# A branch for overflow blocks moved ahead of the last regular block, with its loads on GpSimd's queue, and norm rows spread by products

## The chip, the cores and the metric

The kernel runs on one core of one Trainium2 chip. Its time is the device time of one execution in microseconds (us). The core has five instruction streams: TensorE (PE, whose weight loads have their own row PEld), VectorE (DVE), ScalarE (ACT), GpSimd (POOL) and SyncE (SP). Here SP computes nothing; it issues nearly all transfers from HBM.

## The reference

Two decoder layers on 256 tokens of width 1024, in float32. Layer 0 mixes tokens by block attention, layer 1 by a gated MLP (gMLP); each layer then has a mixture of experts. After each part x is normalised with a row `g` and a row `b`.

```python
def grouped_expert_ffn(xf, expert_id, gates, w1, w3, w2):
    # assignments sorted by expert; each block of rows run by its own expert
    def run_block(args):
        rows, e = args
        h = jax.nn.silu(rows @ w1[e]) * (rows @ w3[e])
        return h @ w2[e]
    ...
def reference(x, ...):
    for i in range(DEPTH):                      # 2 layers
        h = moba_attention(...) if i % 2 == 0 else chunked_gmlp(...)
        x = layer_norm(DEEPNORM_ALPHA * x + h, ln1_g[i], ln1_b[i])
        h = hier_moe(...)                       # 64 experts, 2 per token
        x = layer_norm(DEEPNORM_ALPHA * x + h, ln2_g[i], ln2_b[i])
    return x
```

Each expert has three matrices of 1 MB (w1 and w3, packed as two pieces `w13`, and `w2`). All 64 experts of a layer are read, 201 MB a layer.

## The kernel before

**Slots.** Weights and large activations live in a ring of 24 slots of 8 KB a partition (1 MB each). `slot()` takes the slot that was given up first, `slot(True)` the one given up last. A load into a slot waits until whatever used the slot is done.

**Blocks.** In `moe` expert 0 runs on all tokens; the other 63 are taken four at a time, each on up to 32 gathered rows. That makes NB = 16 regular blocks, numbered 0 to 15, the last one with three experts. A block gathers its rows by one-hot products (`gather`, L625), works out gates (`scatter`, L635), does the up products (`up`, L666), silu and product (`mid`, L674 and L675), a transpose (L756), the down products (L762), copies them out of PSUM (`copy`, L104 on DVE, L106 on ACT in turn), and adds the result to four PSUM banks `acc` by products (`back`, L774). Block b+1 is gathered ahead of block b's down products.

**Overflow.** An expert with more than 32 rows needs more blocks. How many there are is known only at run time, in the last element of the integer tile `li`. Up to four further blocks are written as nested `tc.If` bodies (`tail`, L825), each of them on all engines. With these inputs no such block runs: every engine jumps over the four bodies. The branch stands behind the last regular block (L823 reads the count, L828 branches). Its body holds the loads of the extra experts, so SP branches too. On the path that is not taken each engine waits for its own semaphores (SP for those of its transfers) and advances them as the body would have.

**Order.** A scheduler sets the order within each engine; what is inside a `tc.If` does not mix with what is outside. Instructions of an engine run in that order. `keep_warm(2)` issues two 128x512 products that nobody reads (L115): once in the last block, and in layer 0 once more behind the branch. Then comes the norm: statistics (L192), aggregates (L201), a reciprocal root by POOL (L187), and two passes on DVE (L206 subtracts and multiplies by the g row, L207 multiplies and adds the b row). In layer 0 the result is transposed on PE (L231) and the gMLP's first products (L378) follow. The rows come through `load_ln` (L179, L180): two transfers of 512 KB, each a row of 4 KB repeated to 128 partitions, queued on SP behind the last block's weights.

The helpers `copy`, `bank` and `keep_warm`, and the constants `ones` and `ident`, are defined above these functions; pool psB ("B") has two PSUM banks, psA ("A") two, psY ("Y") four.

Of the kernel before, what the change touches and what calls it, by code (L numbers as in the profile page):

```python
# [16 lines left out]
PSUM = bass.MemoryType.PSUM  # L17
SP = mybir.EngineType.SP

P = 128  # L20
D = 1024
# [8 lines left out]
NE = 64  # L30
# [4 lines left out]
NB = -(-NMAIN // 4)  # L35
NTAIL = 4
NBT = NB + NTAIL
STAT = 8
# [12 lines left out]
def trunk(ctx: ExitStack, tc: tile.TileContext, t, out):  # L51
    nc = tc.nc
# [9 lines left out]

    # Everything of 8 KB a partition lives in these slots, weight pieces and activations alike. A piece takes
    # the slot that was given up first, so that it is loaded as far ahead as the slots reach; what is written
    # shortly after it takes its slot may have the one given up last.
    idle = deque(range(RING))
# [43 lines left out]

    # TensorE's clock falls back when it waits; products that nobody reads keep it up until there is work
    def keep_warm(n):
# [3 lines left out]

# [1 line left out]
    xT_slot = slot()  # L118
# [7 lines left out]

# [1 line left out]
    ident = const.tile([P, P], F32, name="ident")  # L128
# [21 lines left out]
    iota_t = ramp([P, T], [[1, T]], 0, 0, "iota_t")  # L150
    # places of the static blocks' rows, by expert; further down, what keeps them out of the others
    iota_s = ramp([P, CAP * STAT], [[1, CAP * STAT]], FAR, 0, "iota_s")
# [13 lines left out]
    iota80 = ramp([NE, 4 * NBT], [[1, 4 * NBT]], 0, 0, "iota80")  # L166
    # dense: experts run on all tokens; stat: experts whose first block has a place known beforehand
    dense = const.tile([NE, 1], F32, name="dense")
# [8 lines left out]
    def load_ln(g, b, l):  # L177
# [3 lines left out]
        return gb  # L181

    def rsqrt(var):
        ve = small.tile([P, 1], F32, tag="ve", name="ve")
        nc.vector.tensor_scalar(ve, var, EPS, None, op0=OP.add)  # L185
        r = small.tile([P, 1], F32, tag="rs", name="rs")
        nc.gpsimd.tensor_tensor(r, ve, mhalf, op=OP.pow)  # L187
        return r
# [4 lines left out]

    # x <- LN(s) for one tile of tokens, s in two halves; each half goes on to `then` as it is ready
    def after(i):
# [15 lines left out]

    # x <- LN(ALPHA * x + acc)
    def close(x, a, acc, gb, then):
# [21 lines left out]

# [1 line left out]
    def attention(xT_slot, x):  # L237
        xT = by_k(xT_slot)
        with tc.tile_pool(name="att", bufs=1) as att, tc.tile_pool(name="att2", bufs=2) as att2:
# [10 lines left out]
            def qkv(g, w):  # L250
                y = ys[g % 2]
                qT = y[:, 0:1024].rearrange("p (c j t) -> p c j t", c=2, j=2)
                kT = y[:, 1024:1536].rearrange("p (c t) -> p c t", c=2)
                v = y[:, 1536:2048].rearrange("p (a f) -> p a f", a=NT)
                # two heads share the partitions: each has its own copy of q, with zeros for the other's
                nc.gpsimd.memset(qT[64:, :, 0, :], 0.0)
                nc.gpsimd.memset(qT[:64, :, 1, :], 0.0)
                for i in range(2):
                    wt = by_k(w[i])
                    for c in range(2):  # L260
                        ps = bank(psA, "A")
                        for kc in range(KC):
                            nc.tensor.matmul(ps[:, :T], wt[:, kc, c * P:(c + 1) * P], xT[:, kc, :],  # L263
                                             start=(kc == 0), stop=(kc == KC - 1))
                        if i == 0:
                            nc.scalar.mul(qT[:64, c, 0, :], ps[:64, :T], SCALE)
                            nc.scalar.mul(qT[64:, c, 1, :], ps[64:, :T], SCALE)
                        else:
                            nc.vector.tensor_copy(kT[:, c, :], ps[:, :T])
                    drop(w[i])  # L270
                wt = by_k(w[2])
                for a in range(NT):
                    ps = bank(psA, "A")
                    for kc in range(KC):
                        nc.tensor.matmul(ps[:, :256], xT[:, kc, a * P:(a + 1) * P], wt[:, kc, :],
                                         start=(kc == 0), stop=(kc == KC - 1))
                    nc.scalar.copy(v[:, a, :], ps[:, :256])
                drop(w[2])
                return qT, kT, v
# [72 lines left out]

# [1 line left out]
    def gmlp(xT_slot, x):  # L354
        xT = by_k(xT_slot)
        with tc.tile_pool(name="gm", bufs=1) as gm, tc.tile_pool(name="gm2", bufs=2) as gm2:
# [35 lines left out]

            # the first tile of tokens goes ahead while the second is still being closed
            ld = [v_load(cb) for cb in range(2)]
# [89 lines left out]

# [1 line left out]
    def moe(l, xT_slot, x, then):  # L486
        xT = by_k(xT_slot)
        with tc.tile_pool(name="mr", bufs=1) as mr:
# [22 lines left out]

            # the dense experts' first products run while the routing is worked out
            def dense_up(e):
# [63 lines left out]

            # a token's rank among its expert's, and its place if that is in a static block
            ab = new(NE, "ab", BF16)
# [34 lines left out]

            # a block's slot: one-hots (later h and its transpose), gates, gathered rows (later the output)
            def gather(b, m=None):
# [12 lines left out]

            # where a block's rows go back to, and how much they weigh there  # L630
            def scatter(m, oh, xg):
# [10 lines left out]

            def load(src, regs, into=None, parts=1):
                ws = [slot() for _ in regs] if into is None else into
                n = 2048 // parts
                for i in range(parts):
                    for w, e in zip(ws, regs):
                        nc.sync.dma_start(w[:, i * n:(i + 1) * n], src[bass.ds(e, 1), :, i * n:(i + 1) * n])
                return ws

            def block_regs(b):
                n = NMAIN - STARTS[b] if b == NB - 1 else 4
                s0 = STARTS[b]
                if s0 + n <= STAT:
                    return [ND + s0 + j for j in range(n)]
                return [nc.values_load(li[0:1, s0 + j:s0 + j + 1], engines=(SP,), min_val=0, max_val=NE - 1)
                        for j in range(n)]
# [21 lines left out]
            first = gather(0, m0)  # L679
            # each expert's first block after the static ones, and the places there  # L680
            rank, sd = sl, em
# [15 lines left out]
            nc.vector.tensor_add(end, base, ex)  # L697
            # which expert each block is of
            mb = mr.tile([NE, 4 * NBT], F32, name="mb")
# [29 lines left out]
            pa = up(first[2], first_half)  # L729
            # gates  # L730
            dg = new(EG, "dg")
# [19 lines left out]

            # one half of a block's output, and its way back to the tokens
            def down(h, hT, ye, w, gT, first=False, last=False, extra=False):
# [24 lines left out]
            for b in range(NB - 1):  # L778
# [6 lines left out]
                if b == 0:  # L785
                    dw2 = piece(t["w2"][l, 0])
                if b == NB // 2:
                    for a in range(NT):
                        for n in range(2):
                            nc.tensor.matmul(acc[a][n], alpha, x[:, a, n * 512:(n + 1) * 512], start=False, stop=False)  # L790
# [9 lines left out]
                drop(*w2, mine)  # L800

            mine, xg, gT, h, hT, ye = nxt
            regs = block_regs(NB - 1)
# [4 lines left out]
            for n in range(2):  # L808
                for w, e in zip(w2, regs):
                    nc.sync.dma_start(by_c(w)[:, :, n * 512:(n + 1) * 512],  # L810
                                      t["w2"][l, bass.ds(e, 1)].rearrange("e p (c n) -> (e p) c n", c=2)
                                      [:, :, n * 512:(n + 1) * 512])
            gb = load_ln("ln2_g", "ln2_b", l)
            down(h, hT, ye, w2, gT, last=True)
# [5 lines left out]

            # blocks beyond the regular ones
            own = [slot() for _ in range(5)]
            more = nc.values_load(li[0:1, 4 * NBT:4 * NBT + 1], min_val=0, max_val=4 * NBT)  # L823

            def tail(b):  # L825
                if b == NBT:
                    return
                with tc.If(more > STARTS[b] - STAT):  # L828
                    _, xg, gT, h, hT, ye = scatter(*gather(b, own[0]))
                    regs = block_regs(b)  # L830
                    mid(up(xg, lambda half: load(t["w13"][l, half], regs, own[1:]), False), h)
                    down(h, hT, ye, load(t["w2"][l], regs, own[1:]), gT, extra=True)
                    tail(b + 1)
                    if b == NB:
                        for a in early:
                            stats(acc[a], st[a])

            tail(NB)
            if l < DEPTH - 1:
                keep_warm(2)  # L840
            drop(*own)
            last = None
# [70 lines left out]
```

## Time and profile before

| what | us |
|---|---|
| median of 3 runs (lowest, highest) | 1359.46 (1357.36, 1360.37) |
| span of the profiled execution, first to last instruction | 1356.7 |
| PE busy in it | 1248.2 (92%) |
| DVE, ACT, POOL busy | 273.3, 118.8, 16.0 |
| SP's transfers, share of the 16 DMA engines' span | 84.1% |

The profiled execution has no other time of its own than its span, so differences are worked out in the span and laid on the median of the runs; 2.8 us lie between the two. The page's 40 slices show DMA at 420 GB/s through most of both mixtures of experts, and at 127 to 188 GB/s in the gMLP, where PE is busy throughout. In the rows, "x62" counts records; a float32 product leaves two records on PE and two on PEld. An entry such as [2.59 <-PEq L828] is idle time of the engine before the row and what ended it; a q behind an engine's name is its instruction sequencer.

### The profile page before, as it was taken

How to read it: one execution, taken by the hardware profiler on the slowest of the kernel's cores; microseconds unless marked ns; L12 is line 12 of the kernel's file. 1: busy time of each engine (PE TensorE's matmuls, PEld its weight loads, DVE VectorE, ACT ScalarE, POOL GpSimd, SP SyncE). 2: the span in 40 equal slices, each digit the busy share in tenths (PEclk: the TensorE clock that was granted, in tenths of full speed). 3: DMA queues.
4: the chain of work that ended last, by engine and by line, in shares of the span. 5: the costliest groups of instructions: out<-in, count | busy, mean ns of one | idle time of the engine just before them, and what ended most of it. 6: DMA issues, size and time to landing. Idle time of an engine off the chain costs nothing. (4 is left out here: it accounts for less than half of the span.)

```text
span 1356.7 us, 16421 instructions
## 1 busy us (share of the span) xinstructions
PE 1248.2 (92%) x6442; PEld 614.5 (45%) x6442; DVE 273.3 (20%) x721; ACT 118.8 (9%) x273; POOL 16.0 (1%) x45
## 2 busy tenths in 40 slices
PE   8999999988898888889999999999998889888885
PEld 7776554433333333324456666655433324333331
DVE  1322531111111111003231111352111111111102
ACT  1321100000000000001010000020000000000000
POOL 2000000000000000000000000000000000000000
PEclk9999999999999999999999999999999999999998
DMA  9936389999999999998943444449999999999995
GB/s 361 420 148 227 126 336 421 421 421 420 421 422 420 421 422 420 421 388 356 419 175 127 184 152 158 188 157 422 420 421 421 421 421 421 422 421 420 421 420 225
DMA packets 71014, 469.02 MB, mean 346 GB/s; under 512 B 8080, under 2 KB 8080, under 8 KB 16784
## 3 DMA queue, kind: packets, MB, share of 16 engines
q1 hardware_dynamic: 69056, 464.55, 84.1%
q10 hardware_dynamic: 1872, 3.32, 0.7%
q8 instruction: 54, 0.88, 0.3%
q14 instruction: 32, 0.26, 0.1%
HBM read 466.79 MB, written 1.05 MB: 345 GB/s over the span
## 5 line engine op out<-in xcount | busy, mean ns | idle before, releaser
L666 PE MATMUL A<-s,s 128*32 128x512 f32 x2048 | 307.5, 602 | 29.0 <-DMA s<-in_w 29.0
L762 PE MATMUL B<-s,s 128*32 128x512 f32 x1024 | 190.6, 598 | 30.7 <-DMA s<-in_w 15.3
L666 PEld LDWEIGHTS A<-s,s 128*32 128x32 f32 x2048 | 70.9, 110 | 215.2 <-issue 150.1
L625 PEld LDWEIGHTS B<-s,s 128*128 128x128 f32 x1024 | 118.9, 192 | 43.8 <-issue 22.0
L625 PE MATMUL B<-s,s 128*128 128x128 f32 x1024 | 128.7, 280 | 0.0
L774 PE MATMUL Y<-s 128*128 128x512 f32 x256 | 118.9, 606 | 1.9 <-ACT s L106 1.5
L104 DVE COPY s<-B 128x512 f32<-128x512 f32 x64 | 44.2, 691 | 365.5 <-PE B L625 196.8
L762 PEld LDWEIGHTS B<-s,s 128*32 128x32 f32 x1024 | 45.6, 109 | 155.9 <-issue 81.5
L438 PE MATMUL A<-s,s 128*128 128x256 f32 x384 | 90.1, 379 | 0.0
L426 PE MATMUL Y<-s,scr 128*128 128x512 f32 x192 | 87.7, 601 | 0.2 <-DVE scr L460 0.2
L106 ACT COPY s<-B 128x512 f32<-128x512 f32 x64 | 37.5, 586 | 519.7 <-PE B L762 271.4
L774 PEld LDWEIGHTS Y<-s 128*128 128x128 f32 x256 | 45.8, 189 | 75.6 <-issue 63.4
L438 PEld LDWEIGHTS A<-s,s 128*128 128x128 f32 x384 | 71.1, 190 | 17.2 <-issue 9.3
L263 PE MATMUL A<-s,s 128*128 128x256 f32 x256 | 64.0, 396 | 5.4 <-DMA s<-in_wqkv 5.4
L263 PEld LDWEIGHTS A<-s,s 128*128 128x128 f32 x256 | 48.9, 199 | 14.9 <-issue 8.7
L426 PEld LDWEIGHTS Y<-s,scr 128*128 128x128 f32 x192 | 34.7, 190 | 40.0 <-issue 35.2
L675 DVE TENSOR_TENSOR s<-s,A 128x256 f32<-128x256 f32 x32 | 13.4, 420 | 160.8 <-ACT s L674 160.8
L378 PE MATMUL A<-s,s 128*128 128x512 f32 x96 | 43.1, 593 | 0.0
L378 PE MATMUL B<-s,s 128*128 128x512 f32 x96 | 42.8, 592 | 0.0
L611 DVE TENSOR_TENSOR s<-iota_t,sm 128x256 f32<-128x256 f32 (+1 forms) x56 | 21.1, 413 | 102.0 <-PE A L666 102.0
L674 ACT ACTIVATE s<-A 128x256 f32<-128x256 f32 x32 | 12.3, 384 | 307.3 <-PE A L666 291.7
L756 PE MATMUL A<-ident,s 128*128 128x128 f32 x64 | 13.8, 297 | 24.3 <-DVE s L675 24.3
(190 smaller groups left out, 703.8 us busy)
## 6 DMA issues: line engine op xcount, KB each, us to landing
s<-in_w SPq DMA_DIRECT2D x372, 1024.0 KB, 19.8
s<-in_w SPq DMA_DIRECT2D x24, 512.0 KB, 11.3
s<-in_wv SPq DMA_DIRECT2D x12, 1024.0 KB, 11.1
s<-in_wu SPq DMA_DIRECT2D x12, 1024.0 KB, 8.8
s<-in_wout SPq DMA_DIRECT2D x12, 1024.0 KB, 9.1
s<-in_wqkv SPq DMA_DIRECT2D x11, 1024.0 KB, 18.1
s<-in_wo SPq DMA_DIRECT2D x4, 1024.0 KB, 19.9
s<-in_ln_g SPq DMA_DIRECT2D x4, 512.0 KB, 10.8
```

What stands on the lines that cost most here:

```text
L104: nc.vector.tensor_copy(o, i)
L106: nc.scalar.copy(o, i)
L263: nc.tensor.matmul(ps[:, :T], wt[:, kc, c * P:(c + 1) * P], xT[:, kc, :], start=(kc == 0), stop=(kc == KC - 1))
L378: nc.tensor.matmul(ps, xT[:, kc, a * P:(a + 1) * P], by_k4(w[kc // 4])[:, kc % 4, :], start=(kc == 0), stop=(kc == KC - 1))
L426: nc.tensor.matmul(acc[a][h], mx[:, a, :], by_c(wo)[:, i % 2, h * 512:(h + 1) * 512], start=(i == 0), stop=(i == NCH - 1))
L438: nc.tensor.matmul(pu[:, :T], by_k(w)[:, kc, j * P:(j + 1) * P], xT[:, kc, :], start=(kc == 0), stop=(kc == KC - 1))
L611: nc.vector.tensor_tensor(oh[i][:, :, :n], over(at, n), s.to_broadcast([P, NT, n]), op=OP.is_equal)
L625: nc.tensor.matmul(ps[:, k * P:(k + 1) * P], x[:, a, kc * P:(kc + 1) * P], oh[2][:, a, :], start=(a == 0), stop=(a == NT - 1))
L666: nc.tensor.matmul(pa[32 * j:32 * j + 32, :], xg[:, kc, 32 * j:32 * j + 32], by_k4(w[min(j, len(w) - 1)])[:, k, :], start=(kc == 0), stop= ...
L756: nc.tensor.transpose(pt[:, c * P:(c + 1) * P], h[:, c * P:(c + 1) * P], ident)
L762: nc.tensor.matmul(py[32 * j:32 * j + 32, :], hT[:, c, 32 * j:32 * j + 32], by_c(w[min(j, len(w) - 1)])[:, c, n * 512:(n + 1) * 512], star ...
L774: nc.tensor.matmul(acc[a][n], gT[:, a * P:(a + 1) * P], ye[:, n * 512:(n + 1) * 512], start=first, stop=last, skip_group_check=extra)
```

## The change

1. `tail(NB)` and the reservation of its five slots move ahead of block 15's up products. The slots are now the five given up last. The recomputation of statistics inside the body goes, since the statistics now always come after it.
2. The body's transfers and its register loads are issued by GpSimd (POOL) instead of SP.
3. `load_ln` for this norm is replaced by `row_ln` in block 12 (two transfers of 4 KB to one partition) and `spread` in block 13: four products of a column of ones with 512 elements of the row, each copied from PSUM over the 128 partitions of the slot. The register with the count is read in block 12 too.

```diff
+    def row_ln(g, b, l):
+        gb = slot()
+        nc.sync.dma_start(gb[0:1, :D], t[g][l:l + 1, :])
+        nc.sync.dma_start(gb[0:1, D:], t[b][l:l + 1, :])
+        return gb
+
+    def spread(gb):
+        for i in range(4):
+            sl = slice(i * 512, (i + 1) * 512)
+            ps = bank(psB, "B")
+            nc.tensor.matmul(ps, ones[0:1, :], gb[0:1, sl], start=True, stop=True)
+            copy(gb[:, sl], ps)
...
+                if b == NB - 4:
+                    gb = row_ln("ln2_g", "ln2_b", l)
+                    more = nc.values_load(li[0:1, 4 * NBT:4 * NBT + 1], min_val=0, max_val=4 * NBT)
+                if b == NB - 3:
+                    spread(gb)
...
+            own = [slot(True) for _ in range(5)]
+
+            def tail(b):
+                if b == NBT:
+                    return
+                with tc.If(more > STARTS[b] - STAT):
+                    _, xg, gT, h, hT, ye = scatter(*gather(b, own[0]))
+                    regs = block_regs(b, POOL)
+                    mid(up(xg, lambda half: load(t["w13"][l, half], regs, own[1:], dma=nc.gpsimd), False), h)
+                    down(h, hT, ye, load(t["w2"][l], regs, own[1:], dma=nc.gpsimd), gT, extra=True)
+                    tail(b + 1)
+
+            tail(NB)
+            drop(*own)
+
             mine, xg, gT, h, hT, ye = nxt
             regs = block_regs(NB - 1)
             pa = up(xg, lambda half: load(t["w13"][l, half], regs, parts=1 + half))
...
-            gb = load_ln("ln2_g", "ln2_b", l)
             down(h, hT, ye, w2, gT, last=True)
...
-            # blocks beyond the regular ones
-            own = [slot() for _ in range(5)]
-            more = nc.values_load(li[0:1, 4 * NBT:4 * NBT + 1], min_val=0, max_val=4 * NBT)
...
-            tail(NB)
             if l < DEPTH - 1:
                 keep_warm(2)
-            drop(*own)
```

The line numbers after the change are 15 or 16 higher: L666 is L681, L774 is L789, L762 is L777, L115 is L116, L206 is L221.

PE between block 14 and block 15 of layer 0, before (block 14's last products L774, block 15's first, the two unread ones):

```order
L774 MATMUL Y<-s_3195 128x512 x4
L666 MATMUL A<-s_3447,s_3354 32x512
L115 MATMUL A<-ones 128x512 x2
L666 MATMUL A<-s_3448,s_3354 32x512
L666 MATMUL A<-s_3449,s_3354 32x512 x2
```

The same place on PE now; the rows left out are the four bodies, over which PE jumps:

```order
L789 MATMUL Y<-s_3224 128x512 x4
L804 TENSOR_LOAD li
L828 COMPARE_AND_BRANCH
...
L828 UNCONDITIONAL_BRANCH x5
L681 MATMUL A<-s_4069,s_3383 32x512
L116 MATMUL A<-ones 128x512 x2
L681 MATMUL A<-s_4070,s_3383 32x512
L681 MATMUL A<-s_4071,s_3383 32x512 x2
```

The read of the count and the branch now stand between block 14's last product and block 15's first.

PE at the end of layer 0's mixture of experts, before, from block 15's transposes to the gMLP's first products:

```order
L756 MATMUL A<-ident,s_3354 128x128 x2
L762 MATMUL B<-s_3499,s_3354 32x512
L762 MATMUL B<-s_3500,s_3354 32x512
L762 MATMUL B<-s_3501,s_3354 32x512 x2
...
L774 MATMUL Y<-s_3354 128x512 x2
L823 TENSOR_LOAD li
L828 COMPARE_AND_BRANCH
...
L828 UNCONDITIONAL_BRANCH x6
L115 MATMUL A<-ones 128x512 x2
L231 MATMUL B<-ident,s_89 128x128 x8
```

The same stretch now:

```order
L771 MATMUL A<-ident,s_3383 128x128 x2
L116 MATMUL A<-ones 128x512
L777 MATMUL B<-s_4121,s_3383 32x512
L777 MATMUL B<-s_4122,s_3383 32x512
L116 MATMUL A<-ones 128x512
L777 MATMUL B<-s_4123,s_3383 32x512 x2
...
L789 MATMUL Y<-s_3383 128x512 x2
L246 MATMUL B<-ident,s_89 128x128 x8
```

The branch is gone from here, and the second pair of unread products has moved from behind the branch to both sides of the first down products.

SP around its branch in layer 0, before (in_w are expert weights, in_wv the gMLP's):

```order
L810 DMA s_3501<-in_w 128x2x512
L179 DMA s_3508<-in_ln_g 128x1024
L180 DMA s_3508<-in_ln_b 128x1024
L823 TENSOR_LOAD li
L823 ISA x2
L81 DMA s_4218<-in_wv 128x2048
L828 COMPARE_AND_BRANCH
...
L828 UNCONDITIONAL_BRANCH x6
L81 DMA s_4220<-in_wv 128x2048
```

SP around it now:

```order
L663 DMA s_4070<-in_w 128x2048
L828 COMPARE_AND_BRANCH x4
L828 UNCONDITIONAL_BRANCH x5
L663 ISA
L663 DMA s_4071<-in_w 128x2048
```

SP's bodies are empty now and stand among block 15's loads; the gMLP's loads follow the last weights without a branch between them.

## Rows read from the trace of the kernel before

**Rows 1.** Windows: span, busy us per engine, granted clock, DMA share, GB/s

```profile
540.00:560.00 20.00, 16.46 (x73) 4.72 (x74) 1.54 (x3) 0.97 (x2) 0.00 (x0) 1.00 1.01 421
610.00:613.00 3.00, 1.98 (x4) 0.68 (x4) 0.83 (x2) 0.58 (x1) 0.00 (x0) 1.00 0.15 55
613.00:615.50 2.50, 0.29 (x1) 0.30 (x2) 0.69 (x3) 0.00 (x0) 0.55 (x1) 1.00 0.39 52
640.00:700.00 60.00, 60.00 (x141) 26.60 (x140) 11.76 (x17) 5.60 (x9) 0.00 (x0) 1.00 0.87 349
```

**Rows 2.** Timeline, end of layer 0's experts: start, us, engine, line, count, idle before

```profile
586.66 3.70 PE L774 MATMUL Y<-s 128*128 128x512 f32 x8
586.83 0.59 ACT L106 COPY s<-B 128x512 f32<-128x512 f32 x1 [11.23 <-PE B L762]
590.29 1.05 PE L666 MATMUL A<-s,s 128*32 128x512 f32 x2
593.18 8.00 PE L666 MATMUL A<-s,s 128*32 128x512 f32 x62
601.23 0.38 ACT L674 ACTIVATE s<-A 128x256 f32<-128x256 f32 x1 [13.82 <-PE A L666]
603.08 2.76 PE L762 MATMUL B<-s,s 128*32 128x512 f32 x18 [0.52 <-DVE s L757]
610.00 0.59 ACT L106 COPY s<-B 128x512 f32<-128x512 f32 x1 [8.39 <-PE B L762]
610.64 1.98 PE L774 MATMUL Y<-s 128*128 128x512 f32 x4 [0.78 <-ACT s L106]
612.87 0.21 DVE L201 BATCH_NORM_AGGREGATE mv<-st 128x2 f32<-128x12 f32 x1 [0.37 <-DVEq L828]
615.04 1.41 DVE L206 SCALAR_TENSOR_TENSOR s<-Y,mv,s 128x512 f32<-128x512 f32 x2 [1.78 <-PEq L828]
615.21 1.96 PE L115 MATMUL A<-ones 128*128 128x512 f32 x4 [2.59 <-PEq L828]
```

**Rows 3.** Line L828 on PE and SP; line L666 on PE: count, ns min/median/max, starts

```profile
L828 PEldq COMPARE_BRANCH  x2: 3557/3702/3846, 611.3 to 1343.8; - x2
L828 SPq EVENT_SEMAPHORE  x9: 17/17/17, 606.4 to 613.5; - x9
L828 SPq COMPARE_BRANCH  x1: 53/53/53, 601.0 to 601.0; - x1
L666 PEldq EVENT_SEMAPHORE  x1: 51/51/51, 587.5 to 587.5; - x1
```

**Rows 4.** Timeline, end of layer 1's experts

```profile
1320.29 0.59 ACT L106 COPY s<-B 128x512 f32<-128x512 f32 x1 [9.61 <-PE B L762]
1323.76 1.05 PE L666 MATMUL A<-s,s 128*32 128x512 f32 x2
1326.65 7.07 PE L666 MATMUL A<-s,s 128*32 128x512 f32 x62
1345.13 0.70 DVE L192 BATCH_NORM_STATS2 st<-Y 128x6 f32<-128x512 f32 x1 [0.16 <-PE Y L774]
1347.84 1.41 DVE L206 SCALAR_TENSOR_TENSOR s<-Y,mv,s 128x512 f32<-128x512 f32 x2 [1.31 <-PEq L828]
```

**Rows 5.** Windows and timeline where TensorE's granted clock fell, and where not

```profile
358.60:362.00 3.40, 1.09 (x9) 0.29 (x12) 0.28 (x1) 0.00 (x0) 0.00 (x0) 1.00 1.02 422
362.00:365.40 3.40, 3.40 (x20) 0.83 (x13) 0.00 (x0) 0.00 (x0) 0.00 (x0) 0.50 1.01 422
361.28 5.32 PE L666 MATMUL A<-s,s 128*32 128x512 f32 x26 [2.31 <-DMA s<-in_w]
571.55 3.62 PE L666 MATMUL A<-s,s 128*32 128x512 f32 x26 [1.65 <-DMA s<-in_w]
```

**Rows 6.** DMA issues: count, KB each, median us from issue to landing

```profile
br<-in_br ACTq DMA_DIRECT2D x2, 36.0 KB, 6.4
out<-s SPq DMA_DIRECT2D x4, 256.0 KB, 2.0
```

More of the change, by code (lines that the diff above doesn't have):

```diff
@@ L18 @@
 SP = mybir.EngineType.SP
+POOL = mybir.EngineType.Pool
 P = 128
@@ L641, in scatter, with load @@
                 return m, xg, gT, m[:, :256], m[:, 256:512].rearrange("p (c s) -> p c s", c=2), m[:, D:]
-            def load(src, regs, into=None, parts=1):
+            def load(src, regs, into=None, parts=1, dma=nc.sync):
                 ws = [slot() for _ in regs] if into is None else into
@@ L647, in load, with block_regs @@
                     for w, e in zip(ws, regs):
-                        nc.sync.dma_start(w[:, i * n:(i + 1) * n], src[bass.ds(e, 1), :, i * n:(i + 1) * n])
+                        dma.dma_start(w[:, i * n:(i + 1) * n], src[bass.ds(e, 1), :, i * n:(i + 1) * n])
                 return ws
-            def block_regs(b):
+            def block_regs(b, engine=SP):
                 n = NMAIN - STARTS[b] if b == NB - 1 else 4
@@ L655, in block_regs @@
                     return [ND + s0 + j for j in range(n)]
-                return [nc.values_load(li[0:1, s0 + j:s0 + j + 1], engines=(SP,), min_val=0, max_val=NE - 1)
+                return [nc.values_load(li[0:1, s0 + j:s0 + j + 1], engines=(engine,), min_val=0, max_val=NE - 1)
                         for j in range(n)]
@@ L819, in moe @@
                 stats(acc[a], st[a])
-            own = [slot() for _ in range(5)]
-            more = nc.values_load(li[0:1, 4 * NBT:4 * NBT + 1], min_val=0, max_val=4 * NBT)
[L825 to L836, printed above, removed]
-            tail(NB)
             if l < DEPTH - 1:
                 keep_warm(2)
-            drop(*own)
             last = None
```

## The prediction

> **What bounds the kernel now.** I read the page's 40 slices first, then windows, then the timeline at the two ends of the experts' stages, and last the branch line. In both mixtures of experts the transfers set the pace: in a stretch of regular blocks the DMA engines are full at 421 GB/s, and PE waits for pieces in what is left of its 16.46 busy us in 20 [rows 1]. In the gMLP it is the other way round: PE is busy for 60.00 of 60 us while DMA moves 349 GB/s [rows 1]. So anything that delays the gMLP's start passes on whole to the second experts' stage, whose loads wait for the slots that the gMLP gives up, and to the end. Between these stages stand two short stretches that PE and DVE set: from block 14's last product to the norm in layer 0, and the same in layer 1 up to the end. The change works in these two. There the reader is to see three things: block 15's up products run nearly without a wait for weights, 62 records in 7.07 us in layer 1 and 8.00 us in layer 0 [rows 2, 4]; PE's branch takes 3.6 and 3.8 us [rows 3], with PE idle for 2.59 us behind its last products in layer 0 [rows 2]; and DVE's first pass L206 waits for that branch, 1.78 us in layer 0 and 1.31 us in layer 1 [rows 2, 4].
>
> **What the removal gives.** In layer 0 the aggregate started at 612.87 after 0.37 us for DVE's own branch, so it could start at 612.5; with its 0.21 us and one tiny operation L206 comes at about 612.9 in place of 615.04: 2.1 us sooner. In layer 1 the last statistics end at 1345.13 + 0.70 = 1345.83; aggregate and tiny operation put L206 at about 1346.2 in place of 1347.84: 1.6 us sooner. These 3.7 us lie on the path that sets the end, since nothing but DVE and PE work follows.
>
> **What the new place costs.** Call B the time of PE's branch. PE's sequencer runs ahead: an event of line L666 at 587.5 [rows 3] shows it behind block 14's four products at once when ScalarE's copy ended at 586.83 + 0.59 = 587.42 [rows 2]. In the old place the same kind of copy ended at 610.59 and the branch began at 611.3, 0.7 us later, the read of the count included; the first product followed 0.3 us behind the branch's end (611.3 + 3.6 = 614.9, against 615.21) [rows 2, 3]. Laid on block 14: branch from 588.1, first product of block 15 at 588.4 + B, in place of 590.29. The delay is D = B - 1.9. Layer 1 gives the same: copy ended at 1320.88, branch from 1321.6, first product 1321.9 + B in place of 1323.76 [rows 4]. Queued behind the branch is everything PE does in block 15, and DVE, ACT and the end wait for that.
>
> What of D stays: in layer 0, 8.00 - 7.07 = 0.9 us of the up products was waiting for weights that a later start finds landed; in layer 1 nothing is absorbed. In layer 0 the moved pair of unread products adds to PE's work, 0.98 us each (1.96 for two, [rows 2]): the first fills the 0.52 us that PE waited for a copy before L762, the second stands among the down products. Together 0.5 + 0.9 = 1.4 us; in the old place the pair cost nothing, because the transposes behind it waited for DVE anyway.
>
> Layer 0: D - 0.9 + 1.4 - 2.1 = D - 1.6. Layer 1: D - 1.6. Sum: 2D - 3.2 = 2B - 7.0.
>
> **The size of B.** PE's own two branches took 3.6 and 3.8 us, but with the DMA engines nearly empty: 55 and 52 GB/s around the first [rows 1]. In the new place block 15's weights are in flight. The one branch in such traffic is SP's: it started at 601.0 and its next event came at 606.4, 5.4 us later [rows 3]. The upper end comes from small transfers: a load of 36 KB that shared the engines with weights landed after 6.4 us, the stores at the empty end after 2.0 us [rows 6]; 4.4 us more on 3.7 is B = 8.1. Lower end 3.6, since nothing in the new place makes a jump over the same four bodies shorter. I take 5.4, the row nearest in traffic: 2 x 5.4 - 7.0 = 3.8 us.
>
> Whether SP's 5.4 us is a jump or a wait for its transfers the rows leave open. [...]
>
> **The clock.** With B = 5.4 PE stands idle from 586.66 + 3.70 = 590.36 to 593.8, 3.4 us, in both layers. [...] The 2.59 us of idleness behind the old branch cost no clock (613.00 to 615.50 reads 1.00, [rows 1]). [...] I take 1.5 us a layer, 3.0 together; the bounds are 0 and 3.4.
>
> **Costs taken as nothing.** The spread adds four products a layer between blocks 12 and 13, 4 x 0.98 = 3.9 us of PE, and four copies of 0.6 us on DVE and ACT. They lie beside the weight transfers, as PE is paced by DMA there [rows 1], and two blocks follow in which to catch up; with that cover gone it is 3.9 us a layer. Two transfers of 4 KB take the place of two of 512 KB: 1 MB, or 2.5 us at 421 GB/s, leaves SP's queue, but it stood behind the last expert weights, where only gMLP loads followed (layer 0) or nothing (layer 1). SP's branch moves into block 15's loads; its bodies are empty, so it passes without the waits that it had. POOL's bodies are not run, its jump lies far ahead of its next work on the path (the root), and none of its transfers is issued. The branch on ACT and DVE is short and both wait for PE there.
>
> **Sum.** 3.8 + 3.0 = 6.8 us on a span of 1356.7 is 1363.5; on the median of the runs, 1359.5 + 6.8 = 1366.3 us, 0.5% slower.
>
> **The rivals.**
>
> 1. *A quiet price.* [...] Then 2 x 3.7 - 7.0 = 0.4 us, PE is idle for only 1.7 us, and the clock holds: 1359.9, no change. For it: PE's two rows agree within 0.3 us. Against: both are from empty engines. 0.26.
>
> 2. *The freed transfers come back* (the other side, faster). SP's branch drained its queue: from 610.00 to 615.50 the engines moved 52 to 55 GB/s in place of 421 [rows 1], 5.5 x 0.87 = 4.8 us of transfers. If the gMLP or the first blocks behind it waited for weights, loading 4.8 us sooner would shorten them: with B at 3.7, 0.4 - 4.8 = -4.4, or 1355.1; with B at 5.4 and a falling clock it would be 6.8 - 4.8 = 2.0, no change. It decides once PE waits for weights at all in the gMLP. Against it: PE's 60.00 of 60 us. 0.12.
>
> 3. [...] B = 8.1: 2 x 8.1 - 7.0 = 9.2, and the clock falls twice, 3.0: 1371.7. For it: the small load in traffic [rows 6]. Against: SP's 5.4 us, got under the same weights. 0.12. [...]
>
> The forecast itself (B about 5.4, the clock lost in one layer or both) has 0.50.
>
> **How the numbers follow.** About 0.2%, 2.7 us, is what a measurement of this kernel can tell from no change. Rival 2 with the quiet price is faster, 0.12. Rival 1 and the low edge of the forecast (B near 4.5, no clock lost: 2.0 us) are the same: 0.26 + 0.02. The rest of the forecast, 0.48, and rival 3 are slower: 0.60. The forecast's own range is 1361.5 (B 4.5) to 1367.5 (5.4 with 3.4 for the clock, and some more). The range for 8 in 10 leaves out rival 2 and the upper half of rival 3: 1358.5 to 1371.
>
> **What would show it.** Right: PE's branch at 5 to 6 us between blocks 14 and 15 in both layers, block 15's first product 3 to 4 us later against block 14's last, a stretch at granted clock 0.50 behind it, L221 straight behind the aggregate, the gMLP still without waits for weights, and layer 0's gMLP starting some 2 to 4 us later than before. Wrong in size: a branch of 3.7 us (rival 1) or 8 us (rival 3). Wrong in kind: a gMLP or second experts' stage that is shorter than before (rival 2), PE waiting for weights in blocks 13 and 14 because of the spread, or the gMLP's start no later although the branch is longer.

## The result and the profile after

The changed kernel takes 1370.95 us (median of 4 runs, 1369.67 to 1372.21), the kernel before 1359.26 us beside it (4 runs): ratio 1.0091, interval 1.0078 to 1.0104, slower by 11.7 us. The prediction was 6.8 us slower, with a range that ended at 1371.0; the ratio laid on the 1359.46 us that the prediction started from is 1371.8. The profiled execution has a span of 1370.4 us, 13.7 us over that of before; the two spans are single executions, and some 2 us of their difference is not in the medians.

The branch, as its line shows it on SP, DVE and PE (count, ns min/median/max, first and last start), answers to [rows 3]:

```profile
L828 SPq COMPARE_BRANCH  x2: 45/49/53, 581.0 to 1310.6; - x2
L828 DVEq COMPARE_BRANCH  x2: 56/64/72, 587.3 to 1327.7; - x2
L828 PEldq COMPARE_BRANCH  x2: 6028/6055/6082, 589.7 to 1330.1; - x2
```

PE's is the one that costs: 6.0 and 6.1 us, in the very stretch in which the DMA engines are full (393 and 400 GB/s). Windows over the two branches, over the up products behind the first, over the first products of the gMLP and over a stretch inside it (span, busy us of PE, PEld, DVE, ACT, POOL, granted clock, DMA share, GB/s), against [rows 1, 5]:

```profile
589.70:595.80 6.10, 2.17 (x6) 0.62 (x4) 0.00 (x0) 0.00 (x0) 0.00 (x0) 0.94 1.02 393
595.80:601.80 6.00, 5.63 (x10) 1.46 (x14) 0.00 (x0) 0.00 (x0) 0.00 (x0) 0.50 1.04 396
602.00:622.00 20.00, 17.45 (x108) 4.75 (x100) 2.70 (x5) 0.97 (x2) 0.00 (x0) 1.00 1.02 416
625.80:629.00 3.20, 3.20 (x7) 1.40 (x6) 3.13 (x8) 0.86 (x2) 0.55 (x1) 0.50 0.62 245
1330.10:1336.20 6.10, 2.19 (x6) 0.64 (x4) 0.00 (x0) 0.00 (x0) 0.00 (x0) 0.96 1.01 400
```

The granted clock stands at 0.50 for 6.8 us in each layer, from about 1 us ahead of the end of the idle time on (595.0 to 601.8 and 1335.7 to 1342.5), and once more for 3.4 us where the gMLP begins (625.7 to 629.1). The timeline of layer 0, against [rows 2]:

```profile
588.17 3.70 PE L789 MATMUL Y<-s 128*128 128x512 f32 x8
596.17 1.89 PE L681 MATMUL A<-s,s 128*32 128x512 f32 x2 [4.31 <-DMA s<-in_w]
597.99 3.78 PE L116 MATMUL A<-ones 128*128 128x512 f32 x4
...
608.90 0.38 ACT L689 ACTIVATE s<-A 128x256 f32<-128x256 f32 x1 [19.99 <-PE A L681]
610.07 1.02 PE L116 MATMUL A<-ones 128*128 128x512 f32 x2
612.00 1.12 PE L116 MATMUL A<-ones 128*128 128x512 f32 x2
620.37 1.98 PE L789 MATMUL Y<-s 128*128 128x512 f32 x4 [0.78 <-ACT s L107]
622.58 1.40 DVE L221 SCALAR_TENSOR_TENSOR s<-Y,mv,s 128x512 f32<-128x512 f32 x2
624.78 1.49 PE L246 MATMUL B<-ident,s 128*128 128x128 f32 x8 [2.43 <-DVE s L222]
626.13 5.18 PE L393 MATMUL A<-s,s 128*128 128x512 f32 x8
631.15 1.04 PE L246 MATMUL B<-ident,s 128*128 128x128 f32 x8
```

In the first of these idle times, 4.31 us long, a DMA is named, but it was the branch that held PE: it ended at 595.75, and the product started 0.4 us later. In layer 1, where the row names the branch (PEq L828), it ended at 1336.15 and the product started 0.4 us later too. Against [rows 4]:

```profile
1328.75 0.58 ACT L107 COPY s<-B 128x512 f32<-128x512 f32 x1 [9.62 <-PE B L777]
1336.58 1.88 PE L681 MATMUL A<-s,s 128*32 128x512 f32 x2 [4.29 <-PEq L828]
...
1349.42 0.38 ACT L689 ACTIVATE s<-A 128x256 f32<-128x256 f32 x1 [20.09 <-PE A L681]
1358.59 1.99 PE L789 MATMUL Y<-s 128*128 128x512 f32 x4 [0.75 <-ACT s L107]
1361.28 1.40 DVE L221 SCALAR_TENSOR_TENSOR s<-Y,mv,s 128x512 f32<-128x512 f32 x2
1365.54 1.41 DVE L222 SCALAR_TENSOR_TENSOR s<-s,rs,s 128x512 f32<-128x512 f32 x2
```

Four more rows of before, which the sections compared here end on:

```profile
622.10 1.04 PE L231 MATMUL B<-ident,s 128*128 128x128 f32 x8
1333.78 0.39 ACT L674 ACTIVATE s<-A 128x256 f32<-128x256 f32 x1 [12.90 <-PE A L666]
1343.11 1.98 PE L774 MATMUL Y<-s 128*128 128x512 f32 x4 [0.75 <-ACT s L106]
1351.87 1.40 DVE L207 SCALAR_TENSOR_TENSOR s<-s,rs,s 128x512 f32<-128x512 f32 x2
```

Cut at the same events, both traces give the change of each section (us):

| section | layer 0 | layer 1 | predicted, each layer |
|---|---|---|---|
| block 14's last products (layer 1: their copy) to block 15's first product | +4.4 | +4.4 | +3.5 |
| on to the activation L689 | +1.8 | +2.8 | +0.6; +1.5 |
| on to block 15's last products | +2.1 | -0.2 | +1.4; 0 |
| on to L221 | -2.2 | -2.0 | -2.1; -1.6 |
| on to the gMLP's second transposes; to the last L222 | +1.5 | +0.2 | 0 |
| sum | +7.5 | +5.2 | +3.4; +3.4 |

From 622.10 to 1320.29 before and from 631.15 to 1328.75 after it is 698.2 and 697.6 us: the gMLP and the second experts pass the delay on whole. Another 1.5 us stand ahead of block 14 of layer 0 already (588.17 against 586.66); the run without a branch, below, has 1.1 of them too (587.79), so they are not the branch's. In the run without the pair at block 15's start, whose edit stands behind this place, block 14's last products start at 586.89: single executions differ here by as much, and no cause is shown.

### The profile page after: what moved, and what is told of

Its sections match the earlier page's. It is cut to its first block, busy times and chain, and to the rows that moved or that the text cites. A ratio compares the mean times of both kernels' runs of the same rounds, so it can differ in the third digit from the quotient of the medians.

```text
span 1370.4 us, 16468 instructions
## 1 busy us (share of the span) xinstructions
PE 1261.6 (92%) x6458; PEld 620.7 (45%) x6458; DVE 275.3 (20%) x725; ACT 121.0 (9%) x277; POOL 16.0 (1%) x45
## 3 DMA queue, kind: packets, MB, share of 16 engines
HBM read 464.71 MB, written 1.05 MB: 340 GB/s over the span
## 5 line engine op out<-in xcount | busy, mean ns | idle before, releaser
L681 PE MATMUL A<-s,s 128*32 128x512 f32 x2048 | 305.9, 601 | 33.8 <-DMA s<-in_w 29.4
L777 PE MATMUL B<-s,s 128*32 128x512 f32 x1024 | 188.8, 598 | 27.5 <-DVE s L772 14.6
L681 PEld LDWEIGHTS A<-s,s 128*32 128x32 f32 x2048 | 70.4, 110 | 218.8 <-issue 158.7
L105 DVE COPY s<-B 128x512 f32<-128x512 f32 x68 | 47.0, 691 | 372.3 <-PE B L640 191.4
L789 PE MATMUL Y<-s 128*128 128x512 f32 x256 | 119.0, 606 | 2.3 <-ACT s L107 1.5
L777 PEld LDWEIGHTS B<-s,s 128*32 128x32 f32 x1024 | 44.9, 109 | 152.0 <-issue 82.4
L789 PEld LDWEIGHTS Y<-s 128*128 128x128 f32 x256 | 45.8, 189 | 76.0 <-issue 60.9
L393 PE MATMUL A<-s,s 128*128 128x512 f32 x96 | 44.6, 610 | 0.0
L393 PE MATMUL B<-s,s 128*128 128x512 f32 x96 | 42.8, 592 | 0.0
L690 DVE TENSOR_TENSOR s<-s,A 128x256 f32<-128x256 f32 x32 | 13.4, 420 | 144.4 <-ACT s L689 144.4
L689 ACT ACTIVATE s<-A 128x256 f32<-128x256 f32 x32 | 12.3, 383 | 313.6 <-PE A L681 298.0
```

The lines of the kernel that those rows point to most:

```text
L105: nc.vector.tensor_copy(o, i)
L393: nc.tensor.matmul(ps, xT[:, kc, a * P:(a + 1) * P], by_k4(w[kc // 4])[:, kc % 4, :], start=(kc == 0), stop=(kc == KC - 1))
L681: nc.tensor.matmul(pa[32 * j:32 * j + 32, :], xg[:, kc, 32 * j:32 * j + 32], by_k4(w[min(j, len(w) - 1)])[:, k, :], start=(kc == 0), stop= ...
L777: nc.tensor.matmul(py[32 * j:32 * j + 32, :], hT[:, c, 32 * j:32 * j + 32], by_c(w[min(j, len(w) - 1)])[:, c, n * 512:(n + 1) * 512], star ...
L789: nc.tensor.matmul(acc[a][n], gT[:, a * P:(a + 1) * P], ye[:, n * 512:(n + 1) * 512], start=first, stop=last, skip_group_check=extra)
```

## Experiments

The theory after the result: PE's branch costs 3.6 to 3.8 us with the DMA engines near empty (4 to 55 GB/s) and 6.0 to 6.1 us with them full (393 and 400 GB/s); the idle time behind it lets the clock fall; the moved pair of unread products costs the rest. Rivals: the rows' spread, GpSimd's queue, or a price that goes with the code around the branch. The runs were taken in three batches apart from the result's, each on one chip with the kernel before beside them (its medians: 1358.68, 1357.96 and 1358.36 us). A difference between kernels of different batches can be about 1 us off; where it matters, the same stretch of both traces is given too.

**Rows only.** The kernel before with `row_ln` and `spread` alone, at blocks 12 and 13.

```diff
...
+                if b == NB - 4:
+                    gb = row_ln("ln2_g", "ln2_b", l)
+                if b == NB - 3:
+                    spread(gb)
...
-            gb = load_ln("ln2_g", "ln2_b", l)
```

> The kernel before with one part of the change alone: the rows of the norm loaded once and spread by four products each, the branch and its loads as before. Theory (the loss is all in the branch's new place): 1358 to 1361 us; the spread's four products, about 4 x 0.9 us, stand behind block 12's weights where TensorE waits for transfers anyway, and the 1 MB less on SP's queue comes after the last weights. Rival (the spread or its copies stand on the path): 1363 to 1367 us, that is + 2 to 4 us a layer, with TensorE's branch still at 3.6 to 3.8 us.

1358.47 us (10 runs) against 1358.68: ratio 1.0003, interval 0.9993 to 1.0012. The spread is free, as the prediction had it. Its products do leave a stretch at granted clock 0.50 in block 13, which the waits for weights there absorb (rows at the end).

**Queue only.** The kernel before, branch in its old place, overflow loads on GpSimd's queue.

```diff
-                    regs = block_regs(b)
-                    mid(up(xg, lambda half: load(t["w13"][l, half], regs, own[1:]), False), h)
...
+                    regs = block_regs(b, POOL)
+                    mid(up(xg, lambda half: load(t["w13"][l, half], regs, own[1:], dma=nc.gpsimd), False), h)
...
```

> The kernel before with the branch where it was, but the overflow's loads on GpSimd's queue and the expert numbers read there, so that SP no longer sits out the branch: the gMLP's first loads can move while TensorE is in layer 0's branch. Theory (the price of TensorE's branch is set by what the DMA engines carry at that moment): 5.5 to 6.1 us for it in layer 0, 3.5 to 3.9 us in layer 1, where nothing follows; the time + 1 to 5 us, 1360 to 1364. Rival (the price goes with the code that surrounds the branch, not with the transfers): 3.6 to 3.9 us in both layers and 1358 to 1361 us. Second rival (GpSimd's queue costs by itself): a loss in layer 1 too, 1362 or more.

1362.32 us; ratio 1.0023, interval 1.0014 to 1.0033. Its branch line, and windows over the two branches:

```profile
L829 PEldq COMPARE_BRANCH  x2: 3766/4962/6157, 611.3 to 1348.0; - x2
```

```profile
611.30:617.50 6.20, 1.31 (x4) 0.25 (x2) 1.06 (x3) 0.00 (x0) 0.55 (x1) 1.00 1.02 419
1348.00:1351.80 3.80, 1.22 (x3) 0.19 (x1) 1.79 (x5) 0.00 (x0) 0.55 (x1) 0.97 0.02 4
```

One place in the code, one kernel, two prices: 6.16 us at 419 GB/s, 3.77 us at 4 GB/s. The theory holds and the rival that ties the price to the code falls. So SP's wait in the old kernel, with the engines at 52 to 55 GB/s [rows 1], was what kept the old branch of layer 0 at 3.6 us. The time lies in the range of the second rival too (GpSimd's queue costs by itself), but its sign is missing: from block 14's last products to the gMLP's second transposes layer 0 takes 39.5 us against 35.4 before, while layer 1's last block, from block 14's last products to its own, takes 23.0 us in both.

The traces of the kernels before and after also show where the difference arises. While each of their four branches lasts on PE, one transfer of instructions starts, 16 KB on DMA queue 8. In the kernel before, at 43 and 4 GB/s, it starts 1.0 and 1.6 us behind the branch's start; in the changed kernel, at 393 and 400 GB/s, 3.6 us behind it in both layers. It then takes 1.0 to 1.2 us, and the branch ends 1.3 to 1.4 us after its end, in all four. So the changed kernel's branches, 2.5 and 2.2 us longer, differ in the time before this transfer starts, 2.6 and 2.0 us longer. That the branch waits for the transfer is read from this order of events; no run changes it.

**Place only.** The changed kernel with the loads on SP's queue and the broadcast norm rows again.

```diff
-                    gb = row_ln("ln2_g", "ln2_b", l)
...
-                    spread(gb)
...
-                    regs = block_regs(b, POOL)
+                    regs = block_regs(b)
...
+            gb = load_ln("ln2_g", "ln2_b", l)
             down(h, hT, ye, w2, gT, last=True)
```

> The changed kernel with two parts taken back: the overflow's loads on SP's queue again, and the norm's rows loaded with both broadcasts where they were; only the branch's place is new. Theory (the branch costs TensorE 6 us amid transfers, and SP's own branch stands ahead of block 15's weights, so that these start late): TensorE's idle ahead of block 15 grows from 4.3 us to 8 to 20 us a layer, 1378 to 1400 us. Rival (SP's branch and its drain cost nothing, since the weights of block 15 are late in any case): 1369 to 1373 us, as the changed kernel.

1376.68 us; ratio 1.0128, interval 1.0111 to 1.0145: between the two, so both were wrong in size. Its line and windows:

```profile
L825 PEldq COMPARE_BRANCH  x2: 3308/4660/6012, 589.6 to 1335.2; - x2
```

```profile
589.60:592.90 3.30, 2.15 (x6) 0.61 (x4) 0.00 (x0) 0.00 (x0) 0.00 (x0) 1.00 0.21 42
1335.20:1341.20 6.00, 2.18 (x6) 0.63 (x4) 0.00 (x0) 0.00 (x0) 0.00 (x0) 1.00 1.01 421
```

SP's drain makes layer 0's branch cheap (3.3 us at 42 GB/s) and block 15's weights late instead: block 14's last products to block 15's transposes take 25.3 us (588.05 to 613.33) against 21.6 in the changed kernel (588.17 to 609.79). The idle time ahead of block 15 stays 4.27 us because late weights take the branch's place in it: the branch ends at 592.9, the first product starts at 596.02.

**No branch.** The changed kernel without `tail(NB)` and the read of its count.

> The changed kernel without the blocks beyond the regular ones: neither the branch nor what stands in it (for these inputs it runs nothing). Rows of the norm, order of the rest and pools as in the changed kernel. Theory (the loss is the branch of TensorE and the clock that falls in its idle): no idle of 4.3 us ahead of block 15 and no stretch at half clock there, 1355 to 1359 us, so 12 to 16 us under the changed kernel. Rival (most of the loss sits in the spread, the order of the unread products or the loads): 1362 to 1371 us.

1356.96 us; ratio 0.9986, interval 0.9976 to 0.9996: 14.0 us under the changed kernel (13.4 us if each is taken against the kernel before of its own batch). From block 14's last products to block 15's it is 6.7 us less in layer 0 and 7.1 us less in layer 1, and the granted clock reads 1.00 there (590 to 602 us). The branch, with what it does to the clock, is the loss. The fall ahead of the gMLP stays in this trace (0.50 from 619 to 622 us), with no branch near:

```profile
617.71 1.54 PE L246 MATMUL B<-ident,s 128*128 128x128 f32 x8 [2.43 <-DVE s L222]
619.06 5.16 PE L393 MATMUL A<-s,s 128*128 128x512 f32 x8
```

**The pair held behind the last products.** `back` and `down` return the last product (`end`).

```diff
             if l < DEPTH - 1:
-                keep_warm(2)
+                with after(end):
+                    keep_warm(2)
```

> The changed kernel with one edge more: the two unread products after the last block may not be issued before that block's last product into the accumulators. Theory (once the branch stands no longer between them, these products are issued into block 15's own chain, 2.1 us there, and leave TensorE idle for 2.43 us ahead of the gMLP's transposes, after which the clock falls, 1.5 us): 1366.5 to 1368.5 us, 3.5 us under the changed kernel, and no stretch at half clock near 625 us. Rival (the pair lies beside other work where it is now): 1370 to 1372 us, and the fall stays.

1366.46 us; ratio 1.0058, interval 1.0042 to 1.0073: 4.5 us under the changed kernel by the medians, 3.2 us if each is taken against the kernel before of its own batch. From block 14's last products to the gMLP's second transposes the trace takes 3.8 us less (39.1 us against 43.0). Its timeline ahead of the gMLP:

```profile
619.99 1.88 PE L116 MATMUL A<-ones 128*128 128x512 f32 x4
622.58 1.29 PE L246 MATMUL B<-ident,s 128*128 128x128 f32 x8 [0.71 <-DVE s L222]
623.93 3.70 PE L393 MATMUL A<-s,s 128*128 128x512 f32 x8
```

The idle time is 0.71 us instead of 2.43, L393's first eight records take 3.70 us instead of 5.18, and the granted clock reads 1.00 from 625 to 630 us: the theory holds. The branch had been a fence that kept the pair in this place.

**Without the pair at block 15's start.** `keep_warm(2)` behind `up` left out.

> The changed kernel without the two unread products at the start of block 15 (nothing that is read changes). They take 3.78 us a layer there, at half clock, just behind the branch. Theory (the clock stays low for a fixed 6.8 us from its fall, whatever TensorE does in them, so that what goes is the work of the pair, 2.0 us at full clock): 1366 to 1368 us, 4 us under the changed kernel. Rival (the pair is what brings the clock back, so the low stretch gets longer without it and takes the gain): 1369 to 1373 us. Second rival (block 15's weights are late in any case): no change, idle of TensorE in its place.

1364.10 us, 6.9 us under the changed kernel by the medians, 5.6 us if each is taken against the kernel before of its own batch; more than the theory's 4. From block 14's last products to block 15's transposes it is 18.7 us in layer 0 (586.89 to 605.58) and 18.5 in layer 1, 2.9 and 3.2 less, which lies between the pair's 2.0 us at full clock and its 3.78 us at half clock. Block 15's 64 records of L681 take 9.58 and 9.54 us, 1.5 us more than in layer 1 of the run without a branch (0.97 us for the first two, 7.07 us for the others); with the pair, the changed kernel takes 2.6 us more than that run from block 15's first product to the end of the pair. So the rival falls: without the pair the fall costs no more. How long the clock is low these rows do not tell. Why the gain is 1 us a layer above the work of the pair, the runs don't show.

**Four unread products ahead of the branch**, with the pair held as above.

```diff
+            with after(end):
+                keep_warm(4)
             tail(NB)
```

> The changed kernel with the pair after the last block held behind it, as in the run pinned, and four more unread products (3.7 us at full clock) between block 14's last product and the branch. Theory (TensorE's sequencer gets to the branch only some 2 us ahead of the products, as the trace shows it, so the branch is reached that much later): TensorE's idle of 4.3 us stays and comes 3.7 us later, the clock falls all the same, 1373 to 1376 us. Rival (the queue of products holds them all while the sequencer goes on to the branch): the branch starts as early as before, the idle falls under 1 us, the clock stays up in both layers, 1360 to 1365 us.

1364.02 us; ratio 1.0041, interval 1.0026 to 1.0057: the rival is right. Block 15's first product starts 8.1 us behind the start of block 14's last products, against 8.0 us with the held pair alone (596.30 and 588.33): the branch comes no later, and the products run while it lasts:

```profile
588.25 3.70 PE L790 MATMUL Y<-s 128*128 128x512 f32 x8
591.78 3.60 PE L116 MATMUL A<-ones 128*128 128x512 f32 x8
596.35 1.05 PE L681 MATMUL A<-s,s 128*32 128x512 f32 x4 [0.97 <-DMA s<-in_w]
```

The first four records behind the branch take 1.05 us, and the granted clock reads 1.00 in both layers (590 to 602 and 1325 to 1337 us). Against the run with the held pair, of the same batch, that is 2.4 us, with the branch still in the path. From block 14's last products to block 15's transposes layer 0 falls from 21.5 to 19.0 us, layer 1 only from 21.7 to 20.7: PE stands still there for 0.97 us from 1335.1 on, with no engine or transfer named as the cause.

**The branch behind block 4**, with the held pair.

```diff
+                if b == 4 - 2:
+                    more = nc.values_load(li[0:1, 4 * NBT:4 * NBT + 1], min_val=0, max_val=4 * NBT)
...
+                if b == 4:
+                    own = [slot(True) for _ in range(5)]
+                    tail(NB)
+                    drop(*own)
```

> The changed kernel with the pair after the last block held as in the run pinned, and the branch put behind block 4 instead of block 14 (expert numbers and loads on GpSimd's queue as in the changed kernel). Theory (between blocks 4 and 14 TensorE waits for weights in each block, 1 to 2 us, so what the branch costs there is made up before block 15 as long as the transfers go on): the branch still about 6 us, the time 1352 to 1356 us, that of the run without a branch less the 3.5 us of the pair, faster than the kernel before. Rival (while TensorE stands, no slots come free, five more are held by the branch, and the transfers stop): 1358 to 1366 us, the DMA share under 0.95 right behind the branch.

1354.61 us (9 runs) against 1357.96: ratio 0.9973, interval 0.9963 to 0.9983. Faster than both kernels. The branch is no cheaper (6.10 us), and the clock falls to 0.50 behind it:

```profile
L797 PEldq COMPARE_BRANCH  x2: 6099/6099/6099, 285.6 to 1018.6; - x2
```

```profile
292.00:297.00 5.00, 4.89 (x16) 3.25 (x17) 0.00 (x0) 0.00 (x0) 0.00 (x0) 0.50 1.01 416
300.00:330.00 30.00, 28.52 (x193) 12.22 (x191) 5.12 (x13) 2.14 (x4) 0.00 (x0) 1.00 1.01 420
330.00:360.00 30.00, 26.50 (x147) 10.12 (x146) 4.15 (x10) 1.55 (x3) 0.00 (x0) 1.00 1.01 421
```

The transfers go on at 420 GB/s, PE works 28.5 of 30 us behind that stretch and is back to 26.5 of 30, waiting for weights, in the 30 us after. Block 7's last products start at 375.05 us, block 14's at 587.80; without any branch it was 375.06 and 587.79. So PE has made up the branch long before block 15, and DVE no longer waits for it at either end.

**The branch behind block 12.** The same with 12 for 4.

> As the run mid_pinned, with the branch behind block 12 instead of block 4. Theory (what matters is how many blocks that wait for weights come between the branch and block 15: behind block 4, block 5 ended 1.6 us late and blocks 7 and 8 in time again, so two blocks make up most of it): 1354.5 to 1357.5 us, 0.5 to 1.5 us a layer above mid_pinned at block 14's last products. Rival (the slots that come free late stop the loads so near the end): 1359 to 1364 us, with TensorE waiting for weights in block 14 or 15.

1356.20 us; ratio 0.9984, interval 0.9974 to 0.9993. Block 13's last products come late and block 14's in time again:

```profile
561.12 3.70 PE L790 MATMUL Y<-s 128*128 128x512 f32 x8
586.27 3.70 PE L790 MATMUL Y<-s 128*128 128x512 f32 x8
```

(555.7 and 587.8 with the branch behind block 4.) The two stand 25.2 us apart, where regular blocks take 30: PE makes up the loss in one block, whose up products run without a named wait (60 records in 7.06 us). As the rival had it, the transfers dip, to 0.91 of full between 561 and 587 us, and block 15 waits for weights twice (0.23 and 0.25 us); but against the branch behind block 4 the price is 1.6 us by the medians, 1.2 us if each is taken against the kernel before of its own batch, not 4 us or more.

**Behind block 4, without the pair at block 15's start.**

> The run mid_pinned without the two unread products at the start of block 15, 2.0 us a layer at full clock there. Theory (block 15's weights are there in time and the clock is up without the pair): 1350 to 1352 us. Rival (the pair keeps the clock up, as it was put there for; without it TensorE's waits in block 15 let it fall): no gain or a loss, 1354 to 1360 us, with a stretch at half clock between 590 and 625 us.

1354.61 us; ratio 0.9971, interval 0.9960 to 0.9981: the same median as with the pair. The time is the rival's, but not its reason: no fall of the clock shows in the records of block 15, of which two take 1.04 us (1.05 in [rows 2]). From block 14's last products to block 15's transposes 0.6 us is won in layer 0 and 0.1 in layer 1, because waits for weights take the place of the products:

```profile
590.75 6.63 PE L681 MATMUL A<-s,s 128*32 128x512 f32 x50
597.61 1.04 PE L681 MATMUL A<-s,s 128*32 128x512 f32 x2 [0.23 <-DMA s<-in_w]
598.92 1.91 PE L681 MATMUL A<-s,s 128*32 128x512 f32 x12 [0.26 <-DMA s<-in_w]
```

## Why the prediction was right in kind and wrong in size

- **What the removal gives: right.** 2.2 and 2.0 us were predicted as 2.1 and 1.6. The branch behind block 4 keeps this gain without the price.
- **The size of B: too small.** I took SP's 5.4 us; PE's branch took 6.05 us, so D was 4.4 us instead of 3.5 in each layer. The bounds (3.6 to 8.1) held, and the choice of a row in traffic over PE's own quiet rows was right: the runs show 6.0 to 6.2 us at 393 to 421 GB/s, and 3.3 to 3.8 us at 4 to 55 GB/s. SP's row was the wrong one: it was its 5.4 us up to the next event, while the branch itself shows 0.05 us on SP in both kernels. Whether that gap was a jump or a wait was not tested apart; to take it for a jump was my estimate. PE's price under traffic is in no row but those of the changed kernel and the runs.
- **The clock: the step that failed most.** I laid one fall of 1.5 us a layer on the idle time, 3.0 together. No run shows this 1.5: it was my estimate, a little under the 1.7 us between the two rows of 26 records in [rows 5] (5.32 and 3.62 us), as was a fall behind 3.4 us of idle time. Here the clock fell at the end of 4.31 and 4.29 us of idle time, stood at 0.50 for 6.8 us in each layer, not the 3.4 us of that case, and cost 2.7 us in layer 0 (1.8, and the 0.9 that I had right as absorbed) and 2.8 in layer 1, 5.5 together. My upper bound of 1.7 a layer was one case taken for the worst one.
- **The moved pair: half seen.** Its time in block 15's chain was 2.1 us, not 1.4. That it leaves PE idle for 2.43 us ahead of the gMLP, and that the clock falls there too (1.5 us), was not in the prediction at all: a term put at nothing. The rows gave a reason to leave it out, since the 2.59 us of idle time before the pair cost no clock in the old kernel [rows 1, 2]; so the length of the idle time alone does not decide it, and the runs don't show what does. Holding the pair back gave 3.8 us between the same events of layer 0.
- **The other costs taken as nothing: right**, for the spread (rows only), and for SP, DVE, ACT and POOL, whose branches take 0.05 to 0.07 us.
- **Rivals.** The freed transfers did not come back: the gMLP and the second experts are 0.6 us shorter of 698. The quiet price is refuted. The third had the time (1371.7) by accident, with 8.1 us for what takes 6.05; that instructions queue behind weights was not shown, only that their transfer starts later (3.6 us behind the branch's start, against 1.0 and 1.6 us).

In sum: 6.8 predicted, + 1.8 for D, + 2.5 for the clock behind the branch, + 0.7 for the pair, + 1.5 for the gMLP's fall, - 0.5 for the larger gain at L221, makes 12.8; the table's two sums give 12.7, the medians 11.7.

## What to carry to other kernels

A branch that holds its engine for several us (here 6.1 us) belonged where that engine waits for transfers with blocks to come (behind block 4, 1354.6 us), not ahead of the last block, where nothing makes up the loss (1366.5 us with the same held pair); and its price is to be read under the traffic of its new place (here 3.3 to 3.8 us at 4 to 55 GB/s, 6.0 to 6.2 us at 393 to 421 GB/s). Products already queued ran on while the branch lasted: four unread ones just ahead of it (3.60 us) cut the idle time from 4.27 to 0.97 us in layer 0, the granted clock read 1.00, and the time fell by 2.4 us. When a branch is moved, look at what it fenced: here two products went into the chain that it had kept them from.

## What the runs showed that was not expected

The clock fell behind products that left PE no idle time: the spread's eight records. The timeline of the kernel with the rows alone, and windows over the spread and what follows it:

```profile
528.34 3.88 PE L193 MATMUL B<-s,ones 1*128 1x512 f32 x8
532.16 1.82 PE L679 MATMUL A<-s,s 128*32 128x512 f32 x2
```

```profile
528.30:532.20 3.90, 3.90 (x10) 1.37 (x10) 1.39 (x2) 0.59 (x1) 0.00 (x0) 1.00 1.02 424
532.40:535.60 3.20, 3.20 (x10) 1.69 (x9) 0.00 (x0) 0.45 (x1) 0.00 (x0) 0.50 1.03 430
```

PE reads as busy throughout, yet the two records after it take 1.82 us, against 1.05 for such a pair in [rows 2]. In the changed kernel the granted clock falls there too, in both layers: to 0.50 from 533.6 to 537.0 us, 0.9 us behind the spread, and from 1274.3 to 1281.1 us, during it. In the kernel before, which loads the rows by broadcast, it reads 1.00 in both stretches. The traces do not say why; no run was made for it.
